# Two-layer hybrid encoder on one core: keys projected ahead of queries, filling branch products in the projections' banks, last recurrent block kept on chip

## The chip, the core and the metric

The kernel runs on one NeuronCore of a Trainium2 chip. The metric is the device time of one execution in microseconds (us). Engines are named as in the profile: PE is TensorE (matmuls), PEld its weight loads, DVE VectorE, ACT ScalarE, POOL GpSimd, SP SyncE. POOL and SP issue DMAs here, POOL the small copies and reloads, SP the rest.

## What is computed

The input is 512 tokens of 1024 channels and 256 memory tokens. After a layer norm come two layers. Each projects the hidden state `h` with a large `w_in` and runs five mixers side by side on slices of it:

```
o_a = dilated attention, 8 heads, position bias      o_b = recurrence over the tokens, both directions, 8 heads
o_c = grouped attention with rotary positions         o_d = differential attention, 4 heads, position bias
o_m = attention to the memory tokens, 4 heads
y   = sum over branches of  sigmoid(h @ w_gate_i + b_i) * (o_i @ w_branch_i)
h   = layer_norm(alpha * h + y @ w_out)
```

All data is float32. A float32 operand is split into a rounded high part and the rest (hi and lo), and a product is three matmuls: hi by hi, hi by lo, lo by hi.

## The kernel before

**Layout.** The hidden state stands transposed on chip (`hT`, hi and lo, 8 blocks of 128 channels by 512 tokens). One block of a projection (`proj`, L161) loads 128 output columns of a weight in two 256 KB pieces on SP's queue, splits each on ACT (L135) and DVE (L136), and issues 8 x 3 matmuls of 512 columns into one PSUM bank (`gemm3_steps`, L145). Weights use one of two sets of buffers, "r" and "f", two pieces deep each.

**PSUM banks.** There are eight: two `pg` (projections), one `pf`, two `psc` (scores), two `pt` (transposes), one `pm`/`po`. A bank can be written anew when the readers of its last contents have finished.

**Attention.** For a pair of heads, `q_stack` (L418) and `k_stack` (L427) bring a projection from its bank to hi and lo parts. `k_stack` must put each part on the other 64 partitions too, with a DMA on POOL's queue (L434, L436), four in all for a block; a score (L443) needs both `kh` and `kl` complete. In mixers A (L526) and D (L643) the order of the text is: project Q, project K, evacuate both, project V, then bias, scores, softmax (L445), transposes and the product with V (`pv_head`, `pv`), then the silu gate (`silu2`, L347), which is one more projected block. In the first head pair of A, Q and K are projected by halves of the tokens (L165). The memory mixer M (L681 to L702) loads its keys and values from DRAM as one tile `kvm` in a pool of its own, projects Q, and only then stacks the keys.

**Fill.** The gates and branch products for A, C, D and M (`branch_steps`, L369) are cut into steps of three matmuls and pulled in between the other work (`pull`, L403): 0.7 step per score block of C (L621), 0.3 in M (L698), one per step of the recurrence (L1106). For each of eight output blocks a gate takes 24 matmuls in `pf`, a tanh on ACT (L379) writes it to the one buffer `gt`, a branch product takes 12 matmuls (6 for M), again in `pf`, and DVE joins both into `y` (L385; L387 and L389 for later branches). Branch inputs other than A's were spilled to DRAM (`spill`, L358) and are reloaded on POOL's queue (`reload`, L361) into four buffers `o`.

**Recurrence (B).** Blocks are projected into `pg` and read there by ACT and DVE (`mixed`, L730 to L736). Its pool of buffers reuses the space of the attention's pool, so its first writes wait until the attention's last spill has left. The result of head pair p (`finish`, L1054) is split to hi and lo, written to DRAM by two DMAs (L1082, L1085), and reloaded after the recurrence.

**Output stage.** For B's branch the same `branch_steps` run with the gate in `psc` and the product in `pg` (L1134), blocks 0 to 3 in order; each finished `y` block is split for the last product with `w_out` and the layer norm.

**What sets the order.** The program's text gives each instruction a priority (earlier is higher). A scheduler then fixes, before the run, one order for each engine: with modelled durations it puts next the first instruction by priority whose inputs and buffers are ready in its model. So an engine does not follow the text strictly (matmuls of several streams are interleaved), but on the chip each engine keeps the fixed order and waits where the model was too early.

Of the kernel before, what the change touches and what calls it, by code (L numbers as in the profile page):

```python
# [9 lines left out]
F32 = mybir.dt.float32  # L10
# [9 lines left out]
S = 512  # L20
# [32 lines left out]
def encoder_kernel(ctx: ExitStack, tc: tile.TileContext, x, mem, ln_in, rel_bias, w_in, par, w_up, a_up,  # L53
                   d_lambda, w_mem, w_branch, w_gate, w_out, lnp, cst, cossin, onehot, cnt, msk, out):
    nc = tc.nc
# [9 lines left out]
    def ps_f():  # L65
        return pp.tile([128, 512], F32, name="pf", tag="pf", bufs=1)
# [205 lines left out]
    with tc.tile_pool(name="init", bufs=1) as ip:  # L272
        mts, xts = [], []

        def load_x(t):
            xt = ip.tile([128, DM], F32, name="xt", tag="xt", bufs=4)
            nc.sync.dma_start(out=xt, in_=x[t * 128:(t + 1) * 128, :])
            xts.append((xt, t))

        load_x(0)  # L280
        load_x(1)
        gb = load_gb(ip, ln_in)
        load_x(2)
        load_x(3)
        raws = [load_w(w_in[0, b], 1024, ch) for b, ch in zip((0, 4), "rf")]
        for t in range(2):
            mt = ip.tile([128, DM], F32, name="mt", tag="mt", bufs=2)
            nc.sync.dma_start(out=mt, in_=mem[t * 128:(t + 1) * 128, :])
            mts.append(mt)
        layernorm(ip, xts[:2], gb, hT, scr_h)  # L290
        layernorm(ip, xts[2:], gb, hT, scr_h)
        ws0 = [split_w(None, 1024, ch, r) for r, ch in zip(raws, "rf")]
        for t in range(2):
            for j in range(2):
                ps = ps_s()
                for i in range(4):
                    nc.tensor.transpose(ps[:, i * 128:(i + 1) * 128],
                                        mts[t][:, (4 * j + i) * 128:(4 * j + i + 1) * 128], ident)
                sl = slice(t * 128, (t + 1) * 128)
                for i in range(2):  # L300
                    m = mT[2 * j + i]
                    split2(m[:, 0, :, sl], m[:, 1, :, sl], ps[:, 256 * i:256 * i + 256].rearrange("p (k t) -> p k t", k=2))

        rb = ip.tile([32, 12], F32, name="rb", tag="rb")
        nc.sync.dma_start(out=rb, in_=rel_bias)
        oh = ip.tile([32, 1024], F32, name="oh", tag="oh")
        nc.sync.dma_start(out=oh, in_=onehot)
        ct = ip.tile([12, 1024], F32, name="ct", tag="ct")
        nc.sync.dma_start(out=ct, in_=cnt)
        tab = ip.tile([12, 1024], F32, name="tab", tag="tab")  # L310
        for i in range(2):
            ps = ps_m()
            sl = slice(i * 512, (i + 1) * 512)
            mm(ps[0:12, :], rb, oh[:, sl], start=True, stop=True)
            stt(tab[:, sl], ps[0:12, :], -1.0, ct[:, sl], ALU.mult, ALU.subtract)
        nc.sync.dma_start(out=scr_tab, in_=tab)
        for h in range(2):
            toeplitz(h)
        mk = ip.tile([128, NMSK], F32, name="mk", tag="mk")
        nc.sync.dma_start(out=mk, in_=msk)  # L320
        nc.gpsimd.tensor_copy(msk_t, mk)

    nc.sync.dma_start(out=cs_t[:, 128:], in_=cst[:, 128:NCST])
    for l in range(L):
# [9 lines left out]

        ot = []
        y = [None] * 8

        def new_o():
            return big.tile([128, 2, S], F32R, name="o", tag="o", bufs=4)
# [26 lines left out]
                r.append(t)  # L366
            return r

        def branch_steps(br, os, nk, done=None, ch="f", pool=wp, gb=1):  # L369
            k0 = K0[br]  # L370
            if os is None:
                os = reload(br, nk)
            for db in range(8):
                ps = ps_f() if ch == "f" else ps_s()
                w = split_w(w_gate[l, br * 8 + db], 1024, "f")
                yield from gemm3_steps(ps, [(*wk(w, k), hT[:, 0, k, :], hT[:, 1, k, :]) for k in range(8)])
                gt = pool.tile([128, S], F32, name="gt", tag="gt", bufs=gb)
                i = br * 8 + db
                act(gt, ps, AF.Tanh, scale=0.5, bias=hb[:, i:i + 1])  # L379
                ps = ps_f() if ch == "f" else ps_g()  # L380
                w = split_w(w_branch[l, db, :, k0 * 128:(k0 + nk) * 128], nk * 128, ch)
                yield from gemm3_steps(ps, [(*wk(w, k), os[k][:, 0, :], os[k][:, 1, :]) for k in range(nk)])
                if y[db] is None:
                    y[db] = big.tile([128, S], F32, name="y", tag="y", bufs=8)
                    stt(y[db], gt, 1.0, ps, ALU.add, ALU.mult)  # L385
                else:
                    stt(gt, gt, 1.0, ps, ALU.add, ALU.mult)  # L387
                    if done is None:
                        tt(y[db], y[db], gt, ALU.add)  # L389
                    else:  # L390
                        tt(gt, y[db], gt, ALU.add)
                        done(db, gt)
# [17 lines left out]
        with tc.tile_pool(name=f"att{l}", bufs=1) as at:  # L410
# [115 lines left out]
            for hp in range(4):  # L526
                if l == 0:
                    if hp < 3:
                        toeplitz(2 * hp + 2)
                        toeplitz(2 * hp + 3)  # L530
                ps, ps2 = ps_g(), ps_g()
                if hp == 0:
                    proj_halves((ps, ps2), l, (0, 4), hT, "rf", ws0 if l == 0 else None)
                else:
                    proj(ps, l, hp, hT)
                    proj(ps2, l, 4 + hp, hT, "f")
                q = q_stack(ps)
                k = k_stack(ps2)
                ps = ps_g()
                proj(ps, l, 8 + hp, hT)  # L540
                vT = tile_of("vT", [128, S], F32, 1)
                nc.scalar.copy(vT, ps)
                v = v_pair(vT, 4)
                if l == 0 and hp < L:
                    for b in range(4):
                        memory_kv(hp, b)
                of = tile_of("of", [128, S], F32, 2)
                for i in range(2):
                    b = load_bias(2 * hp + i)
                    p4 = []  # L550
                    for qb in range(4):
                        ps = ps_s()
                        score(ps, q, k, i, qb, S)
                        p, _ = softmax(ps, S, b[:, 384 - 128 * qb:896 - 128 * qb])
                        p4.append(p)
                    pv_head(of, p4, 4, lambda kb: v[:, i, kb, :], i)
                g2 = silu2(at, l, 12 + hp, ch="f")
                oA.append(gated(of, g2))
            if l == 0:
                for h in range(8, 12):  # L560
# [66 lines left out]
                spill(2, b, t)  # L627


            with tc.tile_pool(name=f"attd{l}", bufs=1) as ad:  # L630
                lt = ad.tile([128, 4, 64], F32, name="lt", tag="lt")
                nc.sync.dma_start(out=lt, in_=bass.AP(d_lambda.tensor, d_lambda[l].offset, [[0, 128], [64, 4], [1, 64]]))
# [9 lines left out]
                ts(lam[:, 3:4], P("sub"), 0.5 * (1.0 - lam_init), None, ALU.mult)  # L642
                for h in range(4):  # L643
                    ps = ps_g()
                    proj(ps, l, 44 + h, hT)
                    q = q_stack(ps)
                    ps = ps_g()
                    proj(ps, l, 48 + h, hT)
                    k = k_stack(ps)
                    ps = ps_g()  # L650
                    proj(ps, l, 52 + h, hT)
                    vT = tile_of("vT", [128, S], F32, 1)
# [25 lines left out]
                    spill(3, h, t)  # L678


            with tc.tile_pool(name=f"attm{l}", bufs=1) as am:  # L681
                kv = am.tile([128, 4, 256], F32, name="kvm", tag="kvm")
                nc.sync.dma_start(out=kv, in_=scr_kv[l].rearrange("b p t -> p b t"))
                for b in range(2):
                    ps = ps_g()
                    proj(ps, l, 60 + b, hT)
                    q = q_stack(ps)
                    k = k_stack(kv[:, b, :], 256)
                    v = v_pair(kv[:, 2 + b, :], 2)
                    of = tile_of("of", [128, S], F32, 2)  # L690
                    for i in range(2):
                        p4 = []
                        for qb in range(4):
                            ps = ps_s()
                            score(ps, q, k, i, qb, 256)
                            p, _ = softmax(ps, 256, None, (DVE, ACT)[qb % 2])
                            p4.append(p)
                            pull(0.3)  # L698
                        pv_head(of, p4, 2, lambda kb: v[:, i, kb, :], i)
                    g2 = silu2(at, l, 62 + b)  # L700
                    t = gated(of, g2, True)
                    spill(4, b, t)  # L702


        with tc.tile_pool(name=f"rw{l}", bufs=1) as rp:
# [6 lines left out]
            def recurrence():  # L712
# [341 lines left out]
                def finish(p):  # L1054
# [22 lines left out]
                    yield  # L1077
                    g2 = silu2(rp, l, 16 + 14 + p, 1, "ysq")
                    stt(ys, ys, 0.5, g2, ALU.mult, ALU.mult)
                    hi = rp.tile([128, S], F32R, name="yhi", tag="ysq", bufs=1)  # L1080
                    nc.scalar.copy(hi, ys)
                    nc.sync.dma_start(out=scr_o[K0[1] + p, :, 0, :], in_=f(hi))  # L1082
# [29 lines left out]
        with tc.tile_pool(name=f"out{l}", bufs=1) as op:  # L1112
# [18 lines left out]
                wo.append(t)  # L1131

            gb = load_gb(op, lnp[l])
            for _ in branch_steps(1, None, 4, done, "r", op, 2):  # L1134
                pass
            for t in range(4):
                load_z(t)
# [135 lines left out]
```

## Time and profile before

| | |
|---|---|
| median of 3 runs | 2313.18 us (2310.45 to 2315.23) |
| profiled execution, its own time | 2311.92 us |
| span in that execution, first to last instruction | 2310.1 us |
| PE busy, share of the span | 96% |
| DVE, ACT, POOL busy | 75%, 55%, 3% |
| mean granted TensorE clock | 0.991 |
| DMA traffic | 222.58 MB, mean 96 GB/s |

The profile is one execution. Matmuls overlap in a pipeline, so the busy time of PE is not what it would need at its peak; its idle time, and what ended each idle stretch, is what the views on waits list. [...]

### The profile page before, as it was taken

The page shows a single profiled execution, that of the slowest core. Times are in us where ns is not written, and L with a number is a line of the kernel's source. Part 1 is how long each engine was busy: PE and PEld are TensorE (multiplying, and loading weights), DVE is VectorE, ACT ScalarE, POOL GpSimd, SP SyncE. Part 2 cuts the span into 40 slices and gives each one's busy share as a digit, 9 for nine tenths or more (in the row PEclk, how much of TensorE's full clock was granted, in tenths as well). Part 3 has the DMA queues.
Part 4 walks back from the last instruction along what each step waited for, and adds up shares of the span by engine and source line. Part 5 has one row for each costly group of instructions (what it writes and reads, how often), then busy time and mean ns, then how long its engine had stood idle before and what let it go on. Part 6 is the DMA issues. An engine that isn't in the chain of part 4 may idle for free.

```text
span 2310.1 us, 36289 instructions
## 1 busy us (share of the span) xinstructions
PE 2206.5 (96%) x13056; PEld 1690.5 (73%) x13056; DVE 1733.0 (75%) x4236; ACT 1273.5 (55%) x2785; POOL 60.9 (3%) x119
## 2 busy tenths in 40 slices
PE   6999999999999999999999999999999999999998
PEld 5877777777677777776877777777677777777676
DVE  7676886576889797965567778766778979878455
ACT  3555666675655565544235656666675646555440
POOL 0000000000000000000000000000000000000000
PEclk9999999999999999999999999999999999999999
DMA  7733123332222221315334321232312222222350
GB/s 261 230 95 86 64 76 96 105 95 80 73 79 70 93 77 60 108 51 190 101 116 104 94 64 62 94 99 83 114 60 92 74 65 94 72 93 67 100 180 37
DMA packets 112612, 222.58 MB, mean 96 GB/s; under 512 B 13304, under 2 KB 23288, under 8 KB 112048
## 3 DMA queue, kind: packets, MB, share of 16 engines
q1 hardware_dynamic: 102000, 196.14, 26.5%
q0 software_dynamic: 10432, 24.12, 4.1%
q8 instruction: 103, 1.69, 0.3%
q14 instruction: 77, 0.63, 0.1%
HBM read 188.71 MB, written 28.36 MB: 94 GB/s over the span
## 4 chain that ended last, share of the span: by engine, by line
PE 53%; issue 17%; DVE 17%; ACT 7%; DMA 5%; POOL 0%; SPq 0%; DVEq 0%; POOLq 0%; ACTq 0%
PE pg L150 7%; PE pg L151 7%; PE pg L149 7%; PE pf L149 5%; PE pf L150 4%; PE pf L151 4%; PE psc L443 3%; DVE pr L959 2%; DVE W L961 2%; PE po L488 2%; PE pt L469 2%; DVE wlof L136 1%; PE psc L151 1%; PE psc L150 1%; PE psc L149 1%
## 5 line engine op out<-in xcount | busy, mean ns | idle before, releaser
L150 PE MATMUL pg<-hT,whir 128*128 128x512 f32 (+1 forms) x912 | 366.0, 401 | 0.5 <-DVE hT L176 0.5
L149 PE MATMUL pg<-hT,whir 128*128 128x512 f32 (+1 forms) x912 | 364.4, 400 | 1.9 <-DVE q L424 1.6
L151 PE MATMUL pg<-hT,wlor 128*128 128x512 f32 (+1 forms) x912 | 364.3, 399 | 1.7 <-DVE wlor L136 1.7
L136 DVE TENSOR_TENSOR wlor<-wrawr,whir 128x512 fp32r<-128x512 f32 x240 | 163.7, 687 | 123.2 <-ACT whir L135 114.5
L135 ACT CAST whif<-wrawf 128x512 fp32r<-128x512 f32 (+1 forms) x272 | 164.6, 606 | 149.9 <-PE pf L150 87.4
L135 ACT CAST whir<-wrawr 128x512 fp32r<-128x512 f32 x240 | 147.5, 618 | 178.4 <-PE pg L150 111.9
L149 PE MATMUL pf<-hT,whif 128*128 128x512 f32 x512 | 223.0, 435 | 8.9 <-DVE y L385 5.0
L136 DVE TENSOR_TENSOR wlof<-wrawf,whif 128x512 fp32r<-128x512 f32 (+1 forms) x272 | 181.6, 669 | 48.3 <-ACT whif L135 43.1
L150 PE MATMUL pf<-hT,whif 128*128 128x512 f32 x512 | 208.3, 407 | 0.0
L151 PE MATMUL pf<-hT,wlof 128*128 128x512 f32 x512 | 207.7, 406 | 0.0
L151 PEld LDWEIGHTS pg<-hT,wlor 128*128 128x128 f32 x912 | 172.2, 189 | 40.6 <-DVE wlor L136 4.2
L149 PEld LDWEIGHTS pg<-hT,whir 128*128 128x128 f32 x912 | 172.4, 189 | 38.8 <-ACT whir L135 2.6
L150 PEld LDWEIGHTS pg<-hT,whir 128*128 128x128 f32 x912 | 172.2, 189 | 37.8 <-issue 3.6
L176 DVE TENSOR_TENSOR pT<-pt,pT 128x512 fp32r<-128x512 f32 x176 | 114.2, 686 | 36.3 <-ACT pT L175 34.9
L175 ACT CAST pT<-pt 128x512 fp32r<-128x512 f32 x176 | 94.6, 588 | 63.7 <-PE pt L469 62.6
L149 PEld LDWEIGHTS pf<-hT,whif 128*128 128x128 f32 x512 | 97.5, 190 | 41.2 <-DVE gt L387 10.7
L469 PE MATMUL pt<-cst,p 128*128 128x128 f32 x704 | 118.6, 273 | 0.0
L151 PEld LDWEIGHTS pf<-hT,wlof 128*128 128x128 f32 x512 | 97.3, 190 | 22.4 <-issue 1.6
L959 DVE TENSOR_TENSOR pr<-W,U 128x60 f32<-128x60 f32 (+24 forms) x496 | 103.8, 209 | 11.9
L150 PEld LDWEIGHTS pf<-hT,whif 128*128 128x128 f32 x512 | 98.0, 191 | 18.9 <-issue 3.9
L961 DVE TENSOR_TENSOR W<-W,pr 128x60 f32<-128x60 f32 (+24 forms) x496 | 102.8, 207 | 10.8
L469 PEld LDWEIGHTS pt<-cst,p 128*128 128x128 f32 x704 | 89.7, 141 | 27.3 <-DVE p L460 2.9
(324 smaller groups left out, 4836.9 us busy)
## 6 DMA issues: line engine op xcount, KB each, us to landing
wrawr<-in_w_in_dram SPq DMA_DIRECT2D x224, 256.0 KB, 2.8
wrawf<-in_w_gate_dram SPq DMA_DIRECT2D x160, 256.0 KB, 2.8
o<-scr_o POOLq DMA_DIRECT2D x28, 512.0 KB, 4.5
wrawf<-in_w_branch_dram SPq DMA_DIRECT2D x48, 256.0 KB, 2.7
bias<-scr_toe SPq DMA_DIRECT2D x24, 448.0 KB, 3.3
scr_o<-os SPq DMA_DIRECT2D x20, 512.0 KB, 3.1
wrawf<-in_w_in_dram SPq DMA_DIRECT2D x32, 256.0 KB, 3.2
wrawr<-in_w_out_dram SPq DMA_DIRECT2D x32, 256.0 KB, 3.0
```

Of the source, the lines that this page charges most:

```text
L135: nc.scalar.copy(hi, raw)
L136: tt(lo, raw, f(hi), ALU.subtract)
L149: mm(ps, ah, bh, start=(i == 0), stop=False)
L150: mm(ps, ah, bl, start=False, stop=False)
L151: mm(ps, al, bh, start=False, stop=(i == n - 1))
L175: nc.scalar.copy(hi, src)
L176: tt(lo, src, f(hi), ALU.subtract)
L443: mm(ps[:, :nk], q[:, i, sl], part[:, i if g is None else g, :nk], start=(j == 0), stop=(j == 1))
L469: nc.tensor.transpose(pt[:, qb * 128:(qb + 1) * 128], p4[qb][:, kb * 128:(kb + 1) * 128], ident)
L488: mm(po, vwin(kb), pT[:, b, :], start=(kb == 0 and b == 0), stop=(kb == nkb - 1 and b == 1))
L959: tt(pr, W[:, t8, s:s + 1].to_broadcast([128, nt, n]), U[:, s:s + 1, rsl].to_broadcast([128, nt, n]), ALU.mult)
L961: tt(W[:, t8, rsl], W[:, t8, rsl], pr, ALU.add)
```

## The change

Keys are projected before queries in A and D (with the weights' buffer sets exchanged to match), also at the start of the program. In the first head pair of each layer the silu gate's block moves ahead of the scores. Fill's branch products go to `pg`. M's keys and values are loaded earlier, into the two buffers that C used for `qf`, in two DMAs; M has no pool of its own any more, and it stacks keys before it projects Q. The recurrence's last block is split straight into an `o` buffer; its two stores and its reload go, and the output stage takes that block first in each product.

```
-        raws = [load_w(w_in[0, b], 1024, ch) for b, ch in zip((0, 4), "rf")]
+        raws = [load_w(w_in[0, b], 1024, ch) for b, ch in zip((4, 0), "rf")]
...
-        def branch_steps(br, os, nk, done=None, ch="f", pool=wp, gb=1):
+        def branch_steps(br, os, nk, done=None, ch="f", pool=wp, gb=1, order=None):
...
-                ps = ps_f() if ch == "f" else ps_g()
+                ps = ps_g()
...
-                yield from gemm3_steps(ps, [(*wk(w, k), os[k][:, 0, :], os[k][:, 1, :]) for k in range(nk)])
+                yield from gemm3_steps(ps, [(*wk(w, k), o[:, 0, :], o[:, 1, :]) for k, o in zip(order or range(nk), os)])
...
-                    proj_halves((ps, ps2), l, (0, 4), hT, "rf", ws0 if l == 0 else None)
+                    proj_halves((ps2, ps), l, (4, 0), hT, "rf", ws0 if l == 0 else None)
                 else:
-                    proj(ps, l, hp, hT)
-                    proj(ps2, l, 4 + hp, hT, "f")
+                    proj(ps2, l, 4 + hp, hT)
+                    proj(ps, l, hp, hT, "f")
+                k = k_stack(ps2)
                 q = q_stack(ps)
-                k = k_stack(ps2)
...
+                g2 = silu2(at, l, 12 + hp, ch="f") if hp == 0 else None
                 for i in range(2):
...
-                g2 = silu2(at, l, 12 + hp, ch="f")
+                g2 = g2 or silu2(at, l, 12 + hp, ch="f")
...
+            kvm = [tile_of("qf", [128, S], F32, 2).rearrange("p (b t) -> p b t", b=2) for _ in range(2)]
+            for i in range(2):
+                nc.sync.dma_start(out=kvm[i], in_=scr_kv[l, 2 * i:2 * i + 2].rearrange("b p t -> p b t"))
...
                     ps = ps_g()
+                    proj(ps, l, 48 + h, hT)
+                    k = k_stack(ps)
+                    ps = ps_g()
                     proj(ps, l, 44 + h, hT)
                     q = q_stack(ps)
-                    ps = ps_g()
-                    proj(ps, l, 48 + h, hT)
-                    k = k_stack(ps)
...
-                kv = am.tile([128, 4, 256], F32, name="kvm", tag="kvm")
-                nc.sync.dma_start(out=kv, in_=scr_kv[l].rearrange("b p t -> p b t"))
...
+                k = k_stack(kvm[0][:, b, :], 256)
+                v = v_pair(kvm[1][:, b, :], 2)
+                ps = ps_g()
+                proj(ps, l, 60 + b, hT)
+                q = q_stack(ps)
...
+                    if p == 3:
+                        oB.append(finish_o(rp, ys))
+                        return
                     hi = rp.tile([128, S], F32R, name="yhi", tag="ysq", bufs=1)
...
-            for _ in branch_steps(1, None, 4, done, "r", op, 2):
+            for _ in branch_steps(1, oB + reload(1, 3), 4, done, "r", op, 2, (3, 0, 1, 2)):
```

## Rows read from the trace of the kernel before

**Rows 1.** The page: the span, and busy time by engine.

```profile
span 2310.1 us, 36289 instructions
...
PE 2206.5 (96%) x13056; PEld 1690.5 (73%) x13056; DVE 1733.0 (75%) x4236; ACT 1273.5 (55%) x2785; POOL 60.9 (3%) x119
```

**Rows 2.** Waits of PE over the span: us in total, times, longest.

```profile
PE psc L443 <- DMA kl<-kl: 9.0, 9, 3.1
PE pg L149 <- DMA o<-scr_o: 8.4, 2, 5.2
PE pf L149 <- ACT gt L379: 8.3, 14, 1.5
PE psc L443 <- DMA kh<-kh: 6.1, 12, 1.0
...
PE pt L977 <- DVE U L973: 5.3, 4, 1.9
PE pf L149 <- DVE y L385: 5.0, 2, 2.5
PE pf L149 <- DVE gt L387: 3.3, 8, 0.8
```

**Rows 3.** Windows: stretch, length, busy by engine, granted clock, DMA share, rate.

```profile
core 0: us, PE busy (x) PEld busy (x) DVE busy (x) ACT busy (x) POOL busy (x), PEclk, DMA share, GB/s
40.00:60.00 20.00, 17.00 (x104) 14.18 (x102) 11.12 (x23) 10.87 (x23) 2.19 (x4) 1.00 0.93 284
386.00:391.00 5.00, 4.13 (x13) 3.17 (x14) 2.86 (x8) 2.70 (x6) 0.00 (x0) 0.66 0.28 77
529.00:535.00 6.00, 5.17 (x16) 4.12 (x17) 2.05 (x5) 1.37 (x3) 0.00 (x0) 0.72 0.49 175
1069.00:1074.00 5.00, 4.71 (x14) 3.72 (x15) 1.38 (x2) 1.20 (x3) 0.00 (x0) 0.66 0.98 371
1657.00:1663.00 6.00, 5.52 (x24) 4.44 (x24) 2.82 (x11) 1.45 (x4) 0.10 (x1) 1.00 0.50 182
2195.00:2203.00 8.00, 5.44 (x13) 4.29 (x14) 1.77 (x3) 1.62 (x4) 0.00 (x0) 0.57 0.60 228
```

**Rows 4.** Timeline, one head of D, layer 0: ACT and DVE, POOL, then PE.

```profile
371.42 0.58 ACT L423 ACTIVATE q<-pg 64x512 fp32r<-64x512 f32 x1
...
374.66 0.69 DVE L424 SCALAR_TENSOR_TENSOR q<-pg,q 64x512 fp32r<-64x512 f32 x1 [1.70 <-ACT q L423]
...
382.29 0.51 POOL L436 DMA_DIRECT2D kl<-kl  x1 [0.22 <-issue]
...
383.50 0.39 PE L151 MATMUL pg<-hT,wlor 128*128 128x512 f32 x1
383.73 0.40 PE L443 MATMUL psc<-kh,q 128*128 128x512 f32 x1
385.29 0.49 PE L443 MATMUL psc<-kl,q 128*128 128x512 f32 x1 [1.16 <-DMA kl<-kl]
386.78 0.55 PE L443 MATMUL psc<-kh,q 128*128 128x512 f32 x1 [1.00 <-DMA kh<-kh]
```

**Rows 5.** Timeline, attention to recurrence, layer 0: PE, POOL, ACT, DVE.

```profile
529.83 0.50 PE L149 MATMUL pf<-hT,whif 128*128 128x512 f32 x1 [2.52 <-DVE y L385]
...
535.22 0.95 POOL L724 MEMSET WD<- 128x1024 f32 x1 [34.80 <-DMA scr_o<-os]
...
536.42 1.26 ACT L734 ACTIVATE tmp<-pg,cf 128x512 f32<-128x512 f32 x2 [1.24 <-DVE cf L721]
...
538.31 0.50 PE L149 MATMUL pf<-o,whif 128*128 128x512 f32 x1 [1.07 <-ACT gt L379]
...
538.46 1.40 DVE L736 SCALAR_TENSOR_TENSOR tmp<-pg,par,tmp 128x511 f32<-128x511 f32 x2
```

**Rows 6.** Timeline, recurrence to output stage, layer 1: DVE, POOL, PE.

```profile
2184.40 0.68 DVE L1084 TENSOR_TENSOR ys<-ys,yhi 128x512 fp32r<-128x512 f32 x1
...
2189.34 0.54 POOL L365 DMA_DIRECT2D o<-scr_o  x1 [6.04 <-DMA scr_o<-ys]
...
2197.56 0.79 PE L149 MATMUL pg<-o,whir 128*128 128x512 f32 x1 [5.18 <-DMA o<-scr_o]
```

More of the change, by code (lines that the diff above doesn't have):

```diff
@@ L336, in encoder_kernel @@
         y = [None] * 8
+        oB = []
         def new_o():
@@ L678, in encoder_kernel @@
                     spill(3, h, t)
-            with tc.tile_pool(name=f"attm{l}", bufs=1) as am:
-                kv = am.tile([128, 4, 256], F32, name="kvm", tag="kvm")
-                nc.sync.dma_start(out=kv, in_=scr_kv[l].rearrange("b p t -> p b t"))
[L684 to L702, printed above, removed]
+            for b in range(2):
+                k = k_stack(kvm[0][:, b, :], 256)
[3 more added lines that the diff above has]
+                q = q_stack(ps)
+                of = tile_of("of", [128, S], F32, 2)
+                for i in range(2):
+                    p4 = []
+                    for qb in range(4):
+                        ps = ps_s()
+                        score(ps, q, k, i, qb, 256)
+                        p, _ = softmax(ps, 256, None, (DVE, ACT)[qb % 2])
+                        p4.append(p)
+                        pull(0.3)
+                    pv_head(of, p4, 2, lambda kb: v[:, i, kb, :], i)
+                g2 = silu2(at, l, 62 + b)
+                t = gated(of, g2, True)
+                spill(4, b, t)
         with tc.tile_pool(name=f"rw{l}", bufs=1) as rp:
```

## The prediction

> **What bounds the kernel now.** I read the page first: PE is busy 96% of the 2310.1 us span [rows 1]. The change neither adds nor removes a matmul, so what it can win is PE's idle time, 2310.1 - 2206.5 = 103.6 us, and time lost to a lower clock. The second view is the list of waits of PE [rows 2]; it tells what ended each idle stretch. Three of its kinds are what the change is about. Scores wait for the DMAs that copy key parts: 9.0 + 6.1 = 15.1 us. Fill waits for its only bank `pf`, since gate and branch product of one block follow each other there: 8.3 + 5.0 + 3.3 = 16.6 us. And a branch product of the output stage waits for the last reload of a block: 8.4 us in two waits, one a layer. Together 40.1 us. The rest (the start, the last layer norm, waits inside the recurrence such as the 5.3 us for `U`) is not touched.
>
> The third view is the windows [rows 3], for the clock. In dense stretches it is 1.00. [...] PE loses about (1 - clock) x length: 1.7, 1.7, 1.7 and 3.4 us. Two more stretches after key waits in layer 1 look like the first; I price them at 1.7 each. So the three kinds carry another 3 x 1.7 = 5.1 us (keys), 1.7 (fill), 1.7 + 3.4 = 5.1 (reload).
>
> The price of a block of 24 matmuls comes from the spacing of starts, since durations overlap: 383.73 - 383.50 = 0.23 us [rows 4], so 24 take 5.5 us.
>
> **Keys ahead (A and D).** Now only V's block, 5.5 us, lies between the evacuation of K and the scores. In the head shown the fourth copy was issued at 382.29 and the score that needs it began at 386.78, after waits of 1.16 and 1.00 us [rows 4]: the copies need about 2 us more than they get. With Q behind K another 5.5 us of PE work lies between. That is longer than the longest key wait (3.1 us [rows 2]), so the waits should go. The first pair works by halves; there K's block ends only a quarter of the two blocks (2.8 us) earlier, but the silu block moved ahead of the scores adds 5.5. The four copies and their place on POOL's queue relative to each other stay. Q is now evacuated last; its evacuation ran from 371.42 to 374.66 + 0.69, 3.9 us [rows 4], needs no DMA, and has V's 5.5 us above it: nothing. If that cover shrinks (a V block moved ahead by the scheduler), up to 3.9 us a head come back. Bounds: -20.2 us (15.1 and 5.1 of clock) to 0. I take -12 of the waits, because the small ones (12 kh waits, none over 1.0) also stand where the scheduler's model is too early in general, and -3 of the clock: -15.
>
> The same identical schedule shows why I don't take all of the clock: the wait of 2.52 us [rows 5] comes in layer 1 too, and there the clock stayed at 1.00 (1657 to 1663 [rows 3]) while in layer 0 it fell to 0.72. So a fall is not tied to a wait alone. [...]
>
> **Branch products in `pg`.** The waits of 16.6 us fall in two sorts. In each layer one group stands where attention ends: 2.52 us before a gate and 1.07 before its product in layer 0 [rows 5], some 3.6 a layer, 7.2 in all; 9.4 us are spread over the recurrence. Spread, the cure works: a gate finds `pf` free once its tanh is done, and the next gate can run while a product waits for its bank. I take -8 of 9.4.
>
> Where attention ends it doesn't. The two blocks that open the recurrence fill both `pg` banks, and cannot be read: ACT's read starts at 536.42 and DVE's last read of the first at 538.46 + 0.70 = 539.2, because buffers wait for the attention's last spill (POOL at 535.22, released by that DMA) [rows 5]. Now PE spends this time on gates and products in `pf`; then the product has no bank. From 529.83 - 2.52 = 527.3 to 539.2 are 11.9 us. What PE can do without `pg` is one gate (5.5) and about half of the next (2.8), as `gt` is one buffer and the weights are two pieces deep: 8.3, so 3.6 dry, what it is now. The products then queue behind the opened banks, and the clock may fall as now. I take +1.5 a layer, +3 in all, with 0 of the 1.7 of clock. Term: -8 + 3 = -5. Bounds: -18.3 (all of 16.6 and 1.7) and, if products and projections get in each other's way all through the recurrence, +61 (the first rival).
>
> [...]
>
> **Last block on chip.** The wait of 5.18 us ends when a reload issued at 2189.34 lands; that waited 6.04 us for the store of `ys` [rows 6]. The block itself was complete at 2184.40 + 0.68 = 2185.1, and PE had gates to do until 2197.56 - 5.18 = 2192.4. So a block split on chip is there 7 us before it is needed, and both waits (8.4 us) go. Split work on ACT and DVE stays the same; two stores on SP and one reload on POOL go. In exchange the first product starts with this block, so nine matmuls of blocks 0 to 2 (2.1 us) that now run before the recurrence ends come after it: +1 a layer. With 4 of the 5.1 us of clock: -8.4 - 4 + 2 = -10.4. Bounds: -13.5 to 0 (next late would be gate weights, at a DMA share of 0.98 over 1069 to 1074 [rows 3], now with two 256 KB stores and one 512 KB reload less a layer).
>
> **The rest.** M's early load and keys-first only move two small copies and one load to where queues have room; M's scores show no wait among the large ones [rows 2]: nothing. The silu block of layer 0 puts 512 KB ahead of the bias tables on SP's queue, in a stretch where DMA runs at 284 GB/s and a share of 0.93 [rows 3]: 1.8 us, between 0 and that; I take +1.
>
> **Sum.** -15 - 5 - 10.4 + 1 = -29.4 us against the profiled execution's 2311.9: 2282.5. The median of the runs is 1.3 us above that execution, so 2284.
>
> **The rivals.**
> First, and slower: `pg` becomes the bound in the recurrence. There 36 blocks (14 mixed and 4 gates a layer) go through two banks, and a product now holds one of them for four steps. Evacuating two mixed blocks took from 536.42 to 539.86, 1.7 us each [rows 5]. If PE ran dry for all of it, 36 x 1.7 = 61 us. It decides against the change from 24.4 / 36 = 0.7 us a block on, since the other terms are worth 24.4; at 1.0 us it is +36 in place of -5, in sum +11.6: 2325. For it: three users on two banks, and `gt` lets gates run only one ahead. Against: the scheduler places gates in the freed `pf` just then. Chance 0.12.
>
> Second, the order doesn't follow the text: the scheduler pulls V or scores between, so that Q isn't what lies behind K. The term of -15 is 0: 2299. For it: matmuls of several streams are already interleaved; against: keys have the higher priority. Chance 0.12.
>
> Third, fill gives back more: at the end of attention PE does only the one gate, 11.9 - 5.5 = 6.4 dry a layer in place of 3.6, and the spread waits turn into waits for `pg` of equal size: +6 and up to 4 of clock, so +10 in place of -5: 2299. Chance 0.16.
>
> Fourth, everything goes, banks included: -20.2 - 18.3 - 13.5 + 2 = -50: 2263. Chance 0.10.
>
> **How the numbers follow.** The forecast has 0.5. A measurement of this kernel tells about 0.2%, 4.6 us, from no change: 2308.6 to 2317.8. The forecast and the fourth are faster; the second and third lie 10 us from that edge, and I give about a third of their 0.28 to within it: faster 0.80, same 0.08, slower 0.12. The range leaves out the slower rival and most of the unchanged: 2262 to 2307.
>
> **What would show it.** Right: no key wait above 0.5 us in D and in the first pair; no wait for a reload of `o` at the two ends of the recurrence, clock 1.00 there; a remaining stall of 3 to 5 us a layer just before the first read of a mixed block, now in front of a product in `pg`. Wrong: new waits of PE in `pg` for reads by ACT or DVE of mixed or gate blocks (first rival), or key waits as long as now (second). A recurrence stage longer than before in spite of fewer waits for `pf` would make the prediction wrong.

## The result: slower by 1.8%, and the profile after

| | before | after |
|---|---|---|
| median of 4 runs, same chip | 2313.36 us | 2355.6 us (2352.19 to 2359.63) |
| ratio after to before, 95% interval | | 1.0178 (1.0164 to 1.0192) |
| span of the profiled execution | 2310.1 us | 2357.9 us |
| mean granted clock | 0.991 | 0.968 |

The first lines of the page after answer to [rows 1].

```profile
span 2357.9 us, 36242 instructions
## 1 busy us (share of the span) xinstructions
PE 2228.9 (95%) x13056; PEld 1721.7 (73%) x13056; DVE 1744.8 (74%) x4236; ACT 1275.5 (54%) x2785; POOL 59.3 (3%) x117
```

PE has the same 13056 matmuls as before. Its idle time rose from 103.6 to 2357.9 - 2228.9 = 129.0 us, and the same matmuls were busy for 22.4 us longer, at a lower clock (0.968 against 0.991). So the loss is in both. The list of PE's waits says where (us in total, times, longest), against [rows 2]; "..." marks lines left out, here and below.

```profile
PE pt L988 <- ACT U L983: 14.8, 14, 1.6
...
PE pm L92 <- DVE OM L896: 10.8, 8, 2.5
PE psc L881 <- DVE pr L963: 9.4, 2, 4.7
PE pf L149 <- ACT whif L135: 8.9, 8, 1.4
PE pg L149 <- DVE tmp L740: 6.9, 2, 3.5
...
PE pt L1009 <- ACT WD L990: 5.0, 6, 0.8
...
PE pf L151 <- DVE wlof L136: 3.9, 4, 1.5
...
PE pt L1024 <- ACT WA L1012: 2.8, 6, 0.5
...
PE pf L149 <- ACT gt L380: 0.7, 2, 0.4
```

All three kinds of wait that the change was about are gone: no score waits for a DMA of key parts, no product waits for a reload, and the waits for `gt` fell from 8.3 to 0.7 us. In their place stand waits of the recurrence for its own work on ACT and DVE (`U`, `OM`, `pr`, `WD`, `WA`), in which PE has nothing else to do, and waits of gates for their own split weights (`whif`, `wlof`). Lines of the recurrence are 4 higher than before.

The windows of the two recurrences: before, after, and the first experiment below, the same kernel with products back in `pf`.

```profile
529.00:1057.00 528.00, 509.20 (x3733) 381.04 (x3734) 426.66 (x1151) 298.69 (x707) 8.34 (x16) 0.99 0.24 76
1660.00:2185.00 525.00, 506.57 (x3728) 378.59 (x3727) 426.83 (x1149) 299.28 (x707) 8.34 (x16) 0.99 0.24 76
```

```profile
529.00:1084.00 555.00, 513.85 (x3696) 390.48 (x3695) 424.82 (x1131) 292.41 (x696) 6.04 (x11) 0.94 0.22 68
1700.00:2260.00 560.00, 520.58 (x3723) 396.42 (x3723) 429.29 (x1138) 293.15 (x699) 7.11 (x13) 0.94 0.24 79
```

```profile
529.00:1041.00 512.00, 496.42 (x3695) 370.69 (x3695) 419.26 (x1133) 292.85 (x698) 6.64 (x13) 1.00 0.24 75
1650.00:2162.00 512.00, 496.27 (x3695) 371.18 (x3694) 419.42 (x1133) 289.64 (x693) 7.04 (x13) 1.00 0.27 84
```

With products in `pg` these windows are 555 and 560 us long, with products in `pf` 512 and 512. The windows were set by eye, and those of layer 1 start some 26 us late in the last two kernels. Between two fixed instructions, ACT's L749 and the last L1083 on DVE, a recurrence takes 557.6 and 556.1 us with products in `pg` (526.10 to 1083.75, 1673.19 to 2229.32) and 512.4 in both layers with products in `pf` (526.83 to 1039.27, 1624.19 to 2136.64). So it carries 45 + 44 = 89 of the 99 us between the spans of these two kernels (2357.9 and 2258.8). In the kernel before it took 516.0 and 515.4 us. The clock in the windows is 0.94 against 1.00.

### The profile page after: what moved, and what is told of

It reads as the page before. It is cut to its first block, busy times and chain, and to the rows that moved or that the text cites. A ratio compares the mean times of both kernels' runs of the same rounds, so it can differ in the third digit from the quotient of the medians.

```text
span 2357.9 us, 36242 instructions
## 1 busy us (share of the span) xinstructions
PE 2228.9 (95%) x13056; PEld 1721.7 (73%) x13056; DVE 1744.8 (74%) x4236; ACT 1275.5 (54%) x2785; POOL 59.3 (3%) x117
## 4 chain that ended last, share of the span: by engine, by line
PE 63%; DVE 20%; ACT 9%; DMA 5%; issue 3%; SPq 0%; DVEq 0%; ACTq 0%
PE pg L149 11%; PE pg L151 10%; PE pg L150 10%; PE psc L444 4%; PE po L489 3%; PE pt L470 3%; PE pf L151 3%; PE pf L149 3%; PE pf L150 3%; DVE W L965 2%; DVE pr L963 2%; DVE wlof L136 2%; DMA wrawr<-in_w_out_dram 2%; PE pt L1035 1%; PE pt L1024 1%
## 5 line engine op out<-in xcount | busy, mean ns | idle before, releaser
L149 PE MATMUL pf<-hT,whif 128*128 128x512 f32 x512 | 230.3, 450 | 9.7 <-ACT whif L135 8.9
L151 PE MATMUL pf<-hT,wlof 128*128 128x512 f32 x512 | 218.2, 426 | 3.9 <-DVE wlof L136 3.9
L150 PE MATMUL pf<-hT,whif 128*128 128x512 f32 x512 | 212.7, 416 | 0.0
L149 PEld LDWEIGHTS pf<-hT,whif 128*128 128x128 f32 x512 | 101.2, 198 | 37.5 <-ACT whif L135 11.3
L151 PEld LDWEIGHTS pf<-hT,wlof 128*128 128x128 f32 x512 | 102.1, 199 | 31.4 <-DVE wlof L136 5.7
L150 PEld LDWEIGHTS pf<-hT,whif 128*128 128x128 f32 x512 | 101.4, 198 | 18.9 <-issue 3.8
```

What stands on the lines that cost most here:

```text
L149: mm(ps, ah, bh, start=(i == 0), stop=False)
L150: mm(ps, ah, bl, start=False, stop=False)
L151: mm(ps, al, bh, start=False, stop=(i == n - 1))
```

## The experiments

Each time is a median; each ratio is against the kernel before on the same chip. The kernel before stood at 2313.2 to 2315.7 us in all of them.

### First, the parts one by one

**Products back in `pf`**, the rest of the change kept:

```
-                ps = ps_g()
+                ps = ps_f() if ch == "f" else ps_g()
                 w = split_w(w_branch[l, db, :, k0 * 128:(k0 + nk) * 128], nk * 128, ch)
```

> The changed kernel with one part undone: fill's branch products go back to the bank pf. Theory 1 (banks): putting products into pg is what made the recurrence 40 us longer in each layer; with it undone the recurrence takes its old time and the rest of the change keeps what it won before it (some 13.6 us a layer), so 2283 us, between 2272 and 2295. Theory 2 (order): it is the keys-first order and the earlier start of the recurrence that gave the scheduler a worse order there; then this kernel stays slow, above 2335 us.

Measured: 2260.26 us, ratio 0.9763 (0.9748 to 0.9778). This beats both kernels, and is 12 us below the range expected. So all of the loss, and more, hangs on that one line.

**Only that line**, in the kernel before (the same line the other way):

> The kernel before with this part alone: fill's branch products go to pg. Theory 1 (banks): the recurrence alone costs 2 x 40 us and nothing is won ahead of it: 2380 us, between 2360 and 2395. Theory 2 (order): within 10 us of the kernel before, 2303 to 2323.

Measured: 2410.42 us, ratio 1.0408 (1.039 to 1.0425): +96.6 us alone, +95.3 with the rest of the change (2355.6 - 2260.3). The total hardly depends on the other parts (it is above the range expected), but its make-up does: alone, the line brings waits of 19.0 us for the two blocks that open the recurrence (9.57 us in layer 0), with the rest of the change 6.9.

**Only keys first**, in A and D:

```
-        raws = [load_w(w_in[0, b], 1024, ch) for b, ch in zip((0, 4), "rf")]
+        raws = [load_w(w_in[0, b], 1024, ch) for b, ch in zip((4, 0), "rf")]
...
                     ps = ps_g()
+                    proj(ps, l, 48 + h, hT)
+                    k = k_stack(ps)
+                    ps = ps_g()
                     proj(ps, l, 44 + h, hT)
                     q = q_stack(ps)
-                    ps = ps_g()
-                    proj(ps, l, 48 + h, hT)
-                    k = k_stack(ps)
```

> The kernel before with keys projected before queries in A and D, without the earlier silu block. Theory 1 (banks): the key waits of 15.1 us and some clock go: 2296 us, between 2290 and 2302, and the recurrence keeps its length. Theory 2 (order): the recurrence gets longer by tens of us and the sum is above 2335.

Measured: 2286.73 us, ratio 0.988 (0.9861 to 0.9898): -27, more than was expected.

**Only the last block on chip:**

```
+                    if p == 3:
+                        oB.append(finish_o(rp, ys))
+                        return
...
-            for _ in branch_steps(1, None, 4, done, "r", op, 2):
+            for _ in branch_steps(1, oB + reload(1, 3), 4, done, "r", op, 2, (3, 0, 1, 2)):
```

> The kernel before with the last block of the recurrence kept on chip, alone. If the prediction's working for this part holds: the two waits for the reload (8.4 us) and some clock go, 2303 us, between 2299 and 2307. Rival: gate weights come late in their place and the time is within 4 us of the kernel before.

Measured: 2306.6 us, ratio 0.9961 (0.9946 to 0.9976): -7.3.

**Only the silu block of the first pair and the memory mixer:**

```
+                g2 = silu2(at, l, 12 + hp, ch="f") if hp == 0 else None
...
+            kvm = [tile_of("qf", [128, S], F32, 2).rearrange("p (b t) -> p b t", b=2) for _ in range(2)]
...
-            with tc.tile_pool(name=f"attm{l}", bufs=1) as am:
...
+                k = k_stack(kvm[0][:, b, :], 256)
+                v = v_pair(kvm[1][:, b, :], 2)
```

> The kernel before with the two small parts alone: the silu block of the first head pair ahead of the scores, and the memory mixer with its early load, no pool of its own and keys stacked before its queries are projected. If the parts add up, what the others leave of the 2260 kernel's gain must be theirs: 2314 - 27 - 7 - x = 2260, so 2290 to 2300. If the gain comes from the parts together (keys ahead shifts what fill meets), this alone gives 2305 to 2316.

Measured: 2291.69 us, ratio 0.9902 (0.9885 to 0.9918): -22. The parts add up: -27.1 - 7.3 - 22.2 = -56.6 against the -53.6 of all three together. Its list of waits, against [rows 2]:

```profile
PE psc L443 <- DMA kh<-kh: 5.3, 8, 1.1
PE pf L149 <- ACT gt L379: 5.0, 12, 0.7
PE psc L443 <- DMA kl<-kl: 4.4, 9, 1.3
PE pf L149 <- DVE gt L387: 2.9, 8, 0.7
...
PE pt L980 <- DVE U L976: 1.9, 4, 0.7
```

Key waits fell from 15.1 to 9.7, those for `gt` and `U` from 8.3 and 5.3 to 5.0 and 1.9, and the 5.0 us for `y`, where attention ends, have no row any more. How the 22 us divide between the silu block and the memory mixer wasn't tried apart.

### Then, why a product in `pg` costs 96 us

The trace shows the place. Twice for each head pair, eight times a layer, the recurrence passes through a chain of small matmuls (L981, L988, L1009, L1024), each waiting for ACT or DVE (`U`, `RB` in its buffer, `WD`, `WA`). After the change three of the eight passes of a layer run dry, with the same waits each time. In sum, with the 0.46 us for `WA`, they leave PE idle for 29 us; with products in `pf` the same six passes leave 0.2. PE after the change, at the second pair of layer 0 (most matmuls left out):

```profile
789.62 0.40 PE L151 MATMUL pg<-o,wlof 128*128 128x512 f32 x1
789.95 0.69 PE L981 MATMUL pt<-U,NS 32*32 32x32 f32 x32
792.00 0.50 PE L149 MATMUL pf<-hT,whif 128*128 128x512 f32 x1 [1.36 <-ACT whif L135]
792.34 0.39 PE L150 MATMUL pf<-hT,whif 128*128 128x512 f32 x1
794.30 0.24 PE L988 MATMUL pt<-WD,U 32*32 32x32 f32 x2 [1.57 <-ACT U L983]
795.22 0.99 PE L988 MATMUL pt<-WD,U 32*32 32x32 f32 x30 [0.68 <-ACT U L983]
797.04 2.08 PE L1009 MATMUL pt<-Z,WD 128*128 128x128 f32 x8 [0.83 <-ACT WD L990]
799.58 1.75 PE L1024 MATMUL pt<-OM,WA 64*64 64x128 f32 x14 [0.46 <-ACT WA L1012]
801.26 0.79 PE L151 MATMUL pf<-hT,wlof 128*128 128x512 f32 x1
```

The same chain with products in `pf`:

```profile
760.95 0.69 PE L981 MATMUL pt<-U,NS 32*32 32x32 f32 x32
761.58 0.50 PE L149 MATMUL pg<-hT,whir 128*128 128x512 f32 x1
...
762.86 0.39 PE L149 MATMUL pg<-hT,whir 128*128 128x512 f32 x1
...
766.11 0.39 PE L149 MATMUL pf<-o,whif 128*128 128x512 f32 x1
...
768.98 0.69 PE L988 MATMUL pt<-WD,U 32*32 32x32 f32 x32
769.60 0.50 PE L151 MATMUL pg<-hT,wlor 128*128 128x512 f32 x1
```

Here a block in `pg` and a product fill every gap. (So it is in two of the three passes of a layer; the other, at 656 us in layer 0, is filled by a gate.) In the dry stretch above PE has one gate, and of its weights only the hi part is split: two matmuls run, the third (`wlof`) must wait until DVE comes to it behind the recurrence's own work:

```profile
798.34 1.28 DVE L136 TENSOR_TENSOR wlof<-wrawf,whif 128x512 fp32r<-128x512 f32 x2
```

What is the block in `pg`? Its reader tells: the silu gate of the same head pair. With products in `pf`, and after the change:

```profile
823.41 0.60 ACT L353 ACTIVATE g<-pg 128x512 f32<-128x512 f32 x1
```

```profile
855.93 0.59 ACT L353 ACTIVATE g<-pg 128x512 f32<-128x512 f32 x1
```

In the text this block stands well behind the chain. With products in `pf` it starts at 761.58, 62 us before it is read, and ahead of four products whose joins on DVE begin at 771, 789, 805 and 820. With products in `pg` it comes after four of them (794, 818, 834 and 848), and 6 us before it is read, like every silu block of the recurrence in that kernel. That is the first theory, of **turns**: the users of one set of buffers follow one another in the order of the text, so a projection can't be pulled past a product that stands ahead of it. The second is **crowded banks** (too many blocks for two banks), the third a shortage on fill's side: `gt`, or weights.

**The silu block alone held back, with no product in `pg`** (its weights from fill's set):

```
-                    g2 = silu2(rp, l, 16 + 14 + p, 1, "ysq")
+                    g2 = silu2(rp, l, 16 + 14 + p, 1, "ysq", "f")
```

> The kernel with branch products back in pf (2260), with one edit: the silu block of each finished head pair in the recurrence takes its weights from the set that fill uses (f), no longer from the projections' set (r). The banks are those of the 2260 kernel. Theory of turns: users of one set of buffers follow one another in the order of the text, so the silu block, which stands in the text behind three or four fill blocks, can't be pulled forward any more to fill the stretch in which PE waits for the 32 by 32 chain (the 790 to 801 us of the changed kernel); the stretch goes dry again, and the time rises although no product is in pg: 2310 to 2360. Theory of crowded banks (two banks are too few for projections and products): the banks are not touched, so 2255 to 2270.

Measured: 2315.09 us, ratio 1.0003 (0.9991 to 1.0014): +55 on 2260, with banks untouched. The edit does hold the silu blocks back: each of the eight starts some 8 us before it is read. PE's idle time is 2311.6 - 2192.0 = 119.6 us, against 72.5. In part it lies in the same passes of the chain, some 4 us in four of the six; but there and elsewhere PE waits for something else:

```profile
PE pf L149 <- ACT gt L380: 21.1, 16, 2.9
...
PE pf L149 <- DVE y L386: 7.8, 2, 3.9
PE pf L149 <- DVE gt L388: 7.6, 18, 1.0
```

```profile
638.67 0.80 PE L149 MATMUL pf<-hT,whif 128*128 128x512 f32 x1 [3.91 <-DVE y L386]
```

PE waits for its one bank `pf` to be read (in the first experiment 5.1 us for `gt` of ACT, none for `y` and 2.9 for `gt` of DVE); the waits for `U` from L983, 14.8 us after the change, have no row. So silu blocks that run early, eight of 5.5 us each, are worth up to 55 us in the first experiment. That their lateness is what the changed kernel pays for is not shown by it. The edit also puts the silu blocks into fill's own line for weights, so fill's blocks can't pass them either; which of the two costs how much wasn't tried apart.

**The silu block moved in the text** to stand ahead of the products, right behind V, with a buffer of its own:

```
                     yield from project(p, res)
+                    if p:
+                        pairs[p - 1]["g2"] = silu2(rp, l, 16 + 14 + p - 1, 1, "g2r")
...
-                    g2 = silu2(rp, l, 16 + 14 + p, 1, "ysq")
+                    g2 = q["g2"] if p < 3 else silu2(rp, l, 16 + 14 + p, 1, "g2r")
```

> The changed kernel (2356; products in pg) with one edit: in the recurrence the silu block of a head pair is projected in the text right behind V of the next pair and read at once into a buffer of its own, so it stands ahead of the products and its turn comes just where PE runs dry. Theory of turns: most of the loss comes back, 2265 to 2305. Theory of crowded banks: as many blocks still go through the same two banks, 2340 to 2365. Theory that gates get only one block ahead: also 2340 to 2365.

Measured: 2348.63 us, ratio 1.0142 (1.0107 to 1.0178). A miss for the theory of turns, inside the range of the others: 7 of 96 us came back. PE of this kernel shows where the block went:

```profile
644.49 0.41 PE L149 MATMUL pg<-hT,whir 128*128 128x512 f32 x1
...
649.84 0.40 PE L151 MATMUL pg<-hT,wlor 128*128 128x512 f32 x1
...
658.63 0.50 PE L149 MATMUL pf<-hT,whif 128*128 128x512 f32 x1 [0.63 <-ACT whif L135]
660.55 0.24 PE L990 MATMUL pt<-WD,U 32*32 32x32 f32 x2 [1.20 <-ACT U L985]
```

The block ran at once, from 644.49 to 649.84, and was used up when the chain began at 657. By the scheduler's rule it was first by priority and ready. To fill a gap, work must be free to run early and yet come last by priority; standing early in the text isn't the same. That is the reading of this miss; no further run tests it.

**Two buffers `gt` in the recurrence:**

```
-                gt = pool.tile([128, S], F32, name="gt", tag="gt", bufs=gb)
+                gp, gn = (inrec[0], 2) if inrec and ch == "f" else (pool, gb)
+                gt = gp.tile([128, S], F32, name="gt", tag="gt", bufs=gn)
...
+            inrec.append(rp)
             for _ in recurrence():
```

> The changed kernel with two buffers gt in the recurrence in place of one, so that a gate's tanh doesn't wait for the last product to be joined. Theory that gates get only one block ahead: PE has another gate to do when a product waits for its bank, 2270 to 2320. Theories of turns and of crowded banks: what is missing is no buffer for gates, 2340 to 2365.

Measured: 2353.35 us, ratio 1.0164 (1.0143 to 1.0185): a lack of buffers for gates is not the cause.

**Products in `pg` only until the recurrence:**

```
-                ps = ps_g()
+                ps = ps_f() if inrec and ch == "f" else ps_g()
...
+            inrec.append(1)
             for _ in recurrence():
```

> The changed kernel with branch products in pg only up to the end of attention; those that the recurrence pulls go to pf. Both the theory of turns and that of crowded banks put the loss in the recurrence: 2252 to 2270. A theory by which the end of attention carries part of it: 2280 to 2320.

Measured: 2264.27 us, ratio 0.9774 (0.9754 to 0.9794): within the intervals of the two runs, all of the loss is in the recurrence.

**Three banks in turn:**

```
-        return pp.tile([128, 512], F32, name="pg", tag="pg", bufs=2)
+        return pp.tile([128, 512], F32, name="pg", tag="pg", bufs=3)
...
-        return pp.tile([128, 512], F32, name="pf", tag="pf", bufs=1)
+        return pp.tile([128, 512], F32, name="pf", tag="pg", bufs=3)
```

> The changed kernel with pg and pf made into one set of three banks that projections, gates and products use in turn. Theory of crowded banks: any of them can have any of three banks, 2260 to 2320. Theory of turns: now every block of the recurrence stands in line with every block of fill, so nothing can be pulled ahead by more than three blocks: 2345 to 2400.

Measured: 2351.9 us, ratio 1.0157 (1.0132 to 1.0183). A shared set of three banks gives nothing. It isn't a bank more for the same users, though: the gates, which had `pf`, now stand in that line too.

**A bank each**, in the recurrence, with no bank added:

```
-        return pp.tile([128, 512], F32, name="pg", tag="pg", bufs=2)
...
+        if not inrec:
+            i = turn[0] = 1 - turn[0]
+        return pp.tile([128, 512], F32, name="pg", tag="pg%d" % i, bufs=1)
...
-                ps = ps_g()
+                ps = ps_g(1)
                 w = split_w(w_branch[l, db, :, k0 * 128:(k0 + nk) * 128], nk * 128, ch)
```

> The changed kernel (2356) with its two banks pg kept apart in the recurrence: projections always use the first, branch products always the second; gates stay in pf, and no bank is added. Theory of turns: projections no longer stand behind products in the order of the text, so blocks from further on in the text (silu, the next K) can again be pulled into the stretches where PE would run dry, even with one bank: 2255 to 2295. Theory of crowded banks: each stream has fewer banks than before, and a bank that is being read can't be covered by the other: 2345 to 2390.

Measured: 2299.43 us, ratio 0.9935 (0.9916 to 0.9954): 56 of the 96 us are back, though each stream has fewer banks. So it is the sharing that costs, not the number of banks. The time is 4 us above the range of turns, and 39 above 2260. And the trace doesn't show what turns foretold, a projection pulled into the dry stretch. At the second pair:

```profile
780.64 0.50 PE L153 MATMUL pf<-hT,whif 128*128 128x512 f32 x1
...
781.21 0.39 PE L155 MATMUL pf<-hT,wlof 128*128 128x512 f32 x1
...
782.22 0.69 PE L992 MATMUL pt<-WD,U 32*32 32x32 f32 x32
```

```profile
776.00:790.00 14.00, 14.00 (x145) 10.40 (x143) 12.46 (x22) 10.41 (x22) 0.54 (x1) 1.00 0.21 72
```

In the chain, from 776.58 to 787.18, PE has the 24 matmuls of a gate in `pf`, both weight parts ready, and no projection; it isn't idle (window: length, then busy us by engine from PE on, the granted clock third from the end). The silu block of this pair runs at 828.87 and is read at 834.94, as late as after the change, and so it is in the third pair and in layer 1.

**Fill's split weights three pieces deep** in the recurrence (`lo` likewise):

```
-            hi = wp.tile([128, 512], F32R, name="whi" + ch, tag="whi" + ch, bufs=2)[:, :w]
...
+            j, n = (nf[0], 1) if ch == "f" else ("", 2)
+            if ch == "f":
+                nf[0] = (j + 1) % (3 if inrec else 2)
+            wq = inrec[0] if j == 2 else wp
+            hi = wq.tile([128, 512], F32R, name="whi" + ch, tag="whi%s%s" % (ch, j), bufs=n)[:, :w]
```

> The changed kernel with split weights of fill (set f) three pieces deep in the recurrence in place of two. In the dry stretch of 790 to 801 us PE held a gate of which only the hi part of the weights was split. Theory of late weights: with a third piece DVE splits it before the stretch, and the gate fills it: 2270 to 2320. Theory of turns: the gate is one block only, and silu and K stay behind the products: some of the loss comes back at most, 2325 to 2362.

Measured: 2308.68 us, ratio 0.9976 (0.9966 to 0.9985): 47 us back. This is inside the range of late weights (2270 to 2320) and outside that of turns (2325 to 2362): making the gate ready is enough for half of the loss, with the banks shared as before. PE in the same place, with hi and lo ready:

```profile
779.82 0.69 PE L987 MATMUL pt<-U,NS 32*32 32x32 f32 x32
781.37 0.50 PE L155 MATMUL pf<-hT,whif 128*128 128x512 f32 x1 [0.86 <-ACT gt L386]
...
784.04 0.39 PE L157 MATMUL pf<-hT,wlof 128*128 128x512 f32 x1
784.36 0.69 PE L994 MATMUL pt<-WD,U 32*32 32x32 f32 x32
```

**Both of these cures**, the last two edits together:

> The changed kernel with both edits: projections and products each keep to a bank of their own in the recurrence, and fill's split weights are three pieces deep. If turns and late weights are two causes with a price each (56 and 47 us), together they take back all of the 96 us: 2245 to 2270. If both only fill the same dry stretch, the second adds little: 2285 to 2302.

Measured: 2295.49 us, ratio 0.9916 (0.9887 to 0.9946). They don't add up: the second brings 4 us, and the two intervals overlap. Both fill the same dry stretch. But a bank each also leaves projections only one bank, and the control below prices that at 48 us; so this run alone couldn't have come back to 2260 even if the two cures were independent.

**Three pieces with products in `pf`**, the edit of the weights on the kernel of the first experiment:

> The kernel with products in pf (2260) with three weight pieces for fill in the recurrence. If late weights cost by themselves, whatever the bank, 2215 to 2245. If they cost only where nothing else can be pulled into the dry stretch, 2253 to 2265.

Measured: 2263.99 us, ratio 0.978 (0.9758 to 0.9803). Within the intervals nothing is gained: late weights cost nothing where the dry stretch is filled otherwise.

**One bank for the projections, products in `pf`**, the control for a bank each (its first edit on the kernel of the first experiment):

> The kernel with products in pf (2260) with only one of the two banks pg used in the recurrence. It is the control for the run with separate banks (2299): there, projections had one bank too, and the two opening blocks, which wait for attention's last spill, shut it. If the 39 us that the separate banks leave are the price of having one bank for projections: 2285 to 2300. If they are due to products: 2258 to 2270.

Measured: 2308.51 us, ratio 0.9971 (0.9958 to 0.9983): 48 us for the lack of the second bank, with no product in `pg`; that is 8 us above the range expected. So the 39 us that a bank each leaves are within the price of one bank for projections.

**A bank each, only after the opening blocks:**

```
                 ones_bd = C("bones")
+                inrec.append(1)
...
-            inrec.append(1)
             for _ in recurrence():
```

> The changed kernel with separate banks for projections and products, but only after the two opening blocks of the recurrence, which still use both. In the run with separate banks from the start (2299) the first K was read at 546 us, 13 us later than with products in pf (533). If that opening is what was left: 2 layers x 13 us less, 2268 to 2280. If one bank is too few all through the recurrence: 2290 to 2300.

Measured: 2309.98 us, ratio 0.998 (0.997 to 0.999). A miss; the time is even some 10 us above that of a bank each from the start, and why stays open. The run doesn't settle what the opening costs: the first K is read at 543 us, against 546 with a bank each from the start and 533 with products in `pf`, so the edit hardly shortened the opening.

**What follows.** Shown: the loss hangs on one line and lies in the recurrence. It comes from two streams sharing one set of banks, not from too few banks: a bank each, with none added, takes back 56 us, and what that leaves is within the price of one bank for projections. PE is dry in six passes of the chain (29 of the 56.5 us of added idle time). With a bank each, a gate whose weights are ready fills four of them and a product the other two; with three weight pieces (47 us back) a gate fills all but some 1.5 us of each.

Not shown: that lost turns of the silu blocks are what opens these gaps. The silu blocks do start about 60 us before they are read with products in `pf`, and 6 us after the change, and holding them back costs 55 us, but at other waits; a bank each fills the chain without them. Why the gate stands ready there with a bank each, and not in the shared set, stays open, and so does how the whole 96 us divide.

## Why the prediction was wrong

**Branch products in `pg`: the step that failed.** It was -5 and measured +95. The upper bound of +61, of the first rival, was too low, and the rival, given 0.12, was the right side: right in place (the recurrence) and in that `pg` is shared, not in its mechanism. It priced the reading of a full bank, 1.7 us a block. After the change PE waits hardly at all for `pg` in the recurrence: the 6.9 us for L740 are the two openings, and the price is paid in waits for `U`, `OM`, `pr`, `WD`, `WA`, for weights, and in the clock (0.968 against 0.999 with products in `pf`). (The 10.8 us for `OM` are waits for a bank, but for `pm`, which DVE reads late at L896.) The working counted who sits in `pg` when, and never asked what filled PE's gaps meanwhile. In the kernel before, [rows 2] shows that the chain cost little (5.3 us for `U`), and its gaps were full: at 776 to 788 us in layer 0 with 23 matmuls of a projection from further on and a product, in other passes with a gate. Where a wait is small, the work that fills it has to be named, and asked whether after the edit some work still stands ready there.

**What went as said, in part by luck.** The end of attention: a stall was to remain until the opening blocks are read. It did, 6.9 us in two, one a layer, with 3.6 dry us and 1.5 for queueing forecast for each, and a clock of 0.69 in layer 0. But PE waits there with a block of a projection, not with a product. And the size was luck: the working took the reads to start at 536.42 us [rows 5], while in the changed kernel they start at 523.10; with the line alone, where they start at 542.13, the stall is 9.57 us.

```profile
526.00:531.00 5.00, 4.84 (x15) 3.95 (x16) 4.64 (x10) 4.34 (x7) 0.00 (x0) 0.69 0.28 78
```

The forecast of a longer recurrence in spite of fewer waits for `pf`, named as the sign of a wrong prediction, is what the runs show: 558 and 556 us against 516 and 515.

**Keys ahead: -15, measured -27.** The mechanism held: of 15.1 us of waits for key parts none is left in the run of that part alone, and PE's idle time fell by 103.6 - 88.9 = 14.7. The waits were worth more than the -12 taken, and 10.0 us are PE's busy time, 2206.5 to 2196.5, where I had allowed 3 for the clock. The doubt about small waits was needless, and the bound of -20.2 too tight. The mean clock went from 0.991 to 0.993, by (1 - clock) x length an estimated 4.6 us; where the rest of the busy time went is not shown.

**Last block on chip: -10.4, measured -7.3**, within its bounds, with the mechanism as described: no reload wait is left.

**The rest: +1, measured -22.** "Nothing" for the memory mixer and 0 to 1.8 for silu was the second failed step: the working priced only waits in the mixer's own scores, and the load. But waits listed under other names went: `y` at the end of attention, and in layer 1 the waits for `kl`, 7.4 to 2.0 us. Of these, one of 3.06 us stands at the first scores of A, behind the moved silu block; the others that shrank are in D, where the edit moves nothing, and why they shrank is not shown. Part of that overlaps with what keys ahead gains; the three parts together are 3 us less than their sum.

Without the failed line the other terms were too small by 29 us together (-24.4 against -53.6); with the products the sum came out on the wrong side, 72 us from the median (2355.6 - 2284).

## What to carry to other kernels

Before a block of work is put into a buffer set that another stream uses, ask what fills the gaps of the stream's chains now, and whether it can still be there. Here two streams in one set of two banks cost 96 us, each in a bank of its own 39, and all three users in one set of three banks 92. Small waits on a chain that waits for other engines at each step can be a sign of good filler, not of a short chain; list the filler and what lets it run there (bank, weights, inputs) before touching any of these. And measure the parts one by one: here one line of five parts hid a gain of 2.4%.

## What was not expected of the hardware

The clock's share. The two kernels that differ by the one line have the same 13056 matmuls; their spans differ by 99.1 us, of which 129.0 - 72.5 = 56.5 us are idle time of PE and 2228.9 - 2186.3 = 42.6 us longer busy time. The mean granted clock is 0.968 against 0.999, and the gaps that a dry pass of the chain leaves are of 0.5 to 1.6 us each. The stretch below, of the kernel after, lies in the chain of the first pair: PE had waited 1.36 us for weights and 1.57 us for `U` just before, no wait in it is longer than 0.9 us, and the granted clock is 0.50 of full speed all through. In the windows of the recurrence with products in `pf` it is 1.00.

```profile
653.00:661.00 8.00, 6.11 (x50) 4.91 (x50) 7.92 (x15) 3.55 (x9) 0.00 (x0) 0.50 0.24 81
```
